# A two-layer decoder trunk on one core: one tiny quarter-array product behind the products that spread a norm's factor

## The chip, the cores and the metric

The kernel runs on one core of one Trainium2 chip. The metric is the device time of one execution in microseconds (us): the median of three runs before the change is 1049.05 us, the runs lie between 1049.01 and 1049.5 us. A profile is one execution, recorded instruction by instruction.

## What is computed

A trunk of two layers works on 256 tokens of width 1024. Each layer normalises the activations `h` by their root mean square, sends them through four token mixers, merges these by sigmoid gates, adds the result to `h`, normalises again for a feed-forward block with gate, and normalises a third time for a small gated block that is fed from a second input `p`.

```
def _rmsnorm(x, g):
    xf = x.astype(jnp.float32)
    y = xf * lax.rsqrt(jnp.mean(xf * xf, axis=-1, keepdims=True) + NORM_EPS)
    return (y * g.astype(jnp.float32)).astype(x.dtype)
...
for i in range(DEPTH):
    xn = _rmsnorm(h, norm_mix[i])
    u = xn @ w_in[i]
    ...
    h = h + (merged @ w_out[i]).astype(h.dtype)
    hn = _rmsnorm(h, norm_ffn[i])
    ff = (jax.nn.silu(hn @ w_ffn_gate[i]) * (hn @ w_ffn_up[i])) @ w_ffn_down[i]
    h = h + ff.astype(h.dtype)
    hp = _rmsnorm(h, norm_ple[i])
    ple = jax.nn.sigmoid(hp @ w_ple_gate[i]) * (p[i] @ w_ple_proj[i])
    h = h + ple.astype(h.dtype)
return _rmsnorm(h, norm_final)
```

## The kernel before

**Layout.** Features lie on the 128 partitions and the 256 tokens along the free axis. A weight tile of 128x1024 is loaded by one DMA of 512 KB from SyncE's queue (L210) and split in two parts: ScalarE writes the rounded part `wh` (L211), and VectorE, or for some tiles GpSimd, writes the rest `wl` (L212). There are four buffers for the raw tile and three for each part. The activations are split the same way into `xh` and `xl`.

**The big products.** One block of 128x128 weights times 128x256 activations takes three products that add up in PSUM: `wl` with `xh`, `wh` with `xl`, `wh` with `xh`. They are issued in `mm3` (L226, L227, L228), in `gemm_pair` where the last blocks of the input come late (L261, L262, L263), and in L430 to L432 for a token-major projection. All of them fill the whole array and stream 256 columns. In each layer the input projection (w_fm), the gates and branches (w_gate, w_branch), the output projection (w_out), the feed-forward (w_fg, w_fu, w_fd) and the last gate (w_pg) follow in this order on TensorE, each accumulation of 8, 16 or 22 blocks behind the other. TensorE executes in the order of its list.

**The small products.** The mixers work on chunks and heads with products on parts of the array (64x64, 128x64, 32x32 and others). They go through a helper `Front`, whose line L141 issues them ahead of the big ones as soon as they can be done, so that the big products fill the gaps.

**A norm.** The gain is multiplied into `xh` and `xl`, the factor `rsqrt(mean)` only after the products. `h_stat` makes this factor while TensorE goes on with products that don't need it yet. The squares are summed over partitions by products with a column of 1/1024 (L354, one column out). VectorE makes the inverse root (L285 to L299). Two products (L359) with the identity matrix spread the 2 x 128 factors over all partitions into 256 columns of a PSUM tile `pB` of 512 columns, and ScalarE copies them out (L365 of the old numbering, tile `rstd`). VectorE multiplies `rstd` into what leaves the projections. `h_stat` runs seven times: once for x, and in each layer behind the mixers (it makes the feed-forward's factor), behind the feed-forward (the last block's factor) and behind the last block (the next layer's mixers' factor, in the second layer that of the output).

**The order** of each engine's list is made by the framework when the kernel is built: it simulates the program and takes, among the instructions that are ready, the one with the lowest priority number. A change in one place can therefore move instructions elsewhere.

Of the kernel before, what the change touches and what calls it, by code (L numbers as in the profile page):

```python
# [32 lines left out]
P = 128  # L33
L = 2
T = 256
# [115 lines left out]
class Trunk:  # L151
# [193 lines left out]
                add(sq[:, 0], sq[:, 0], sq[:, 1])  # L345
                self.accs.pop()

    def h_stat(self, last=False):
        nc = self.nc
        ps = self.ps([P, 512], "pB")  # L350
        n = len(self.accs)
        for i, a in enumerate(self.accs):
            for tc_ in range(2):
                nc.tensor.matmul(ps[:, tc_:tc_ + 1], a[:, tc_ * P:(tc_ + 1) * P], self.inv_dm,  # L354
                                 start=i == 0 and tc_ == 0, stop=i == n - 1, skip_group_check=True)
        self.rt = self.rsqrt(ps[:, 0:2], 2, 1.0, EPS)
        bc = self.ps([P, 512], "pB")
        for tc_ in range(2):
            nc.tensor.matmul(bc[:, tc_ * P:(tc_ + 1) * P], self.rt[:, tc_:tc_ + 1].to_broadcast([P, P]), self.ident,  # L359
                             start=True, stop=True)  # L360
        self.rstd_ps = bc[:, None, :T].to_broadcast([P, 2, T])
        if last:
            return
        self.rstd = self.t([P, T], "rstd")
        nc.scalar.activation(self.rstd, bc[:, :T], AF.Copy)  # L365
        self.rstd_b = self.rstd[:, None, :].to_broadcast([P, 2, T])
# [820 lines left out]
    def body(self):  # L1187
        self.wcount = 0

        self.shared = False  # L1190
        self.tc.cur_priority += Front.AHEAD
        self.xp = [None] * 4
        self.stream = "B"

        self.lo_plan = list("VVVVV")
        self.setup()
        for p in range(4):
            for c in range(2):
                self.h_done(2 * p + c, lambda c: self.vec[0][:, V_MIX + c:V_MIX + c + 1], first=True)
            if p == 2:  # L1200
                self.ahead.append(self.w_tiles([self.ins["w_fm"][0, 7]], 2))
                self.nc.sync.dma_start(self.h[:, 6:8], self.ins["x"][:, 6:8])
        self.h_stat()
        for l in range(L):
            self.layer(l)

        hn = [self.g([P, 2, T], "A") for _ in range(4)]
        with self.tc.issue_after(self.last_sq.ins):
            for ch in range(8):
                self.nc.scalar.activation(hn[ch // 2][:, ch % 2], self.h[:, ch], AF.Copy,  # L1210
                                          scale=self.vec[0][:, V_NF + ch:V_NF + ch + 1])
        for p in range(4):
            o = self.g([P, 2, T], "B")
            for cs in (slice(0, 1), slice(1, 2)) if p == 0 else (slice(0, 2),):
                self.nc.vector.tensor_mul(o[:, cs], hn[p][:, cs], self.rstd_ps[:, cs])
                self.nc.sync.dma_start(self.out[:, 2 * p + cs.start:2 * p + cs.stop], o[:, cs])
# [34 lines left out]
    def layer(self, l):  # L1251
        nc = self.nc
# [28 lines left out]
        with lane("G"):  # L1281
            kv, ksw, q = self.nsa_in(l)
# [63 lines left out]
        for p in range(4):  # L1346
# [3 lines left out]
            for c, ps in parts:  # L1350
# [3 lines left out]
                for ts in halves:  # L1354
# [4 lines left out]
                    (G if adders[p] == "P" else V).tensor_add(hc, dc, hc)  # L1359
                    for i in range(n):  # L1360
                        self.h_done(2 * p + c + i, gcol, part=ts if len(halves) > 1 else None)
        self.h_stat(l + 1 == L)

    def residual(self, src, xs, gcol, tag=None):

        V = self.nc.vector
        for p in range(4):
            for c, ps in self.pair([src(2 * p + c) for c in range(2)], xs, 2 if p == 0 and len(xs) == 8 else 0, split=p == 3):
                n = ps.shape[1]
                hc = self.h[:, 2 * p + c:2 * p + c + n]  # L1370
                V.scalar_tensor_tensor(hc, ps, 0.5, hc, op0=OP.mult, op1=OP.add)
                for i in range(n):
                    self.h_done(2 * p + c + i, gcol, tag)
        self.h_stat()

# [89 lines left out]
```

## Time and profile before

| | |
|---|---|
| median of three runs | 1049.05 us |
| the profiled execution | 1048.63 us |
| its span, first to last instruction | 1046.9 us |
| TensorE products recorded | 9520 |
| VectorE busy | 738.5 us (71%) |
| ScalarE busy | 542.9 us (52%) |
| GpSimd busy | 240.2 us (23%) |
| DMA moved | 171.32 MB, mean 164 GB/s |

Busy time of an engine is the union of its instructions' records. A product's end is modelled by the profiler, and in a stream the records overlap (records of 0.28 us start 0.11 to 0.12 us apart); so what a product costs there is the distance between the starts of neighbours, not the length of its record. A product of two plain 32-bit operands appears as two records: L359 stands twice in each of the seven norms and shows 28 records. A row that names a helper's line (L141, L211, L226) collects all calls of the helper.

### The profile page before, as it was taken

The numbers are of one execution on the slowest core, as the hardware profiler recorded it, in microseconds if no ns is written. First come the engines' busy times: TensorE is split into PE (matmuls) and PEld (weight loads), VectorE is DVE, ScalarE is ACT, GpSimd is POOL, SyncE is SP. The second block draws the span as 40 slices with busy tenths as digits, with TensorE's granted clock in tenths as the row PEclk, the third lists the DMA queues.
The fourth block names the chain that finished last, engine by engine and source line by source line (L and its number), as shares of the span: only waits on it lengthen the run. The fifth ranks groups of instructions, "written<-read, shape, count | busy, mean of one in ns | idle before, by whom it ended". The sixth has DMA issues, their size and how long they took to land.

```text
span 1046.9 us, 22801 instructions
## 1 busy us (share of the span) xinstructions
PE 1026.3 (98%) x9520; PEld 986.2 (94%) x9520; DVE 738.5 (71%) x1216; ACT 542.9 (52%) x863; POOL 240.2 (23%) x154
## 2 busy tenths in 40 slices
PE   9999999999999999999899999999999999999996
PEld 9988988899999999999898999988999999999996
DVE  6888968766677667554878999576567676665456
ACT  6644555555654444444555545556556555444444
POOL 0000000044442242232510000000544432332322
PEclk9999999999999999999999999999999999999998
DMA  8654334256665656666544553333565656656551
GB/s 293 193 182 159 90 98 121 68 172 186 190 202 171 198 177 188 186 183 192 168 158 135 179 166 100 110 93 101 182 197 179 198 166 195 191 175 198 171 179 56
DMA packets 50502, 171.32 MB, mean 164 GB/s; under 512 B 5856, under 2 KB 6624, under 8 KB 50272
## 3 DMA queue, kind: packets, MB, share of 16 engines
q1 hardware_dynamic: 50112, 169.76, 52.2%
q8 instruction: 74, 1.21, 0.5%
q14 instruction: 28, 0.23, 0.1%
q10 hardware_dynamic: 288, 0.11, 0.0%
HBM read 168.80 MB, written 1.05 MB: 162 GB/s over the span
## 4 chain that ended last, share of the span: by engine, by line
PE 85%; DVE 9%; ACT 2%; issue 2%; DMA 1%; POOL 1%; DVEq 0%; ACTq 0%; POOLq 0%
PE mm L226 21%; PE mm L227 21%; PE mm L228 21%; PE pB L141 6%; PE pA L141 5%; DVE wl L212 3%; PE pA L226 2%; PE pA L227 2%; PE pA L228 2%; PE pA L262 1%; PE pA L261 1%; PE pA L263 1%; DMA T<-in_w_cmp_dram 1%; ACT wh L211 1%; DVE T L1358 1%
## 5 line engine op out<-in xcount | busy, mean ns | idle before, releaser
L211 ACT ACTIVATE wh<-wr 128x1024 fp32r<-128x1024 f32 (+3 forms) x314 | 325.6, 1040 | 347.0 <-PE mm L228 240.4
L212 DVE TENSOR_TENSOR wl<-wr,wh 128x1024 fp32r<-128x1024 f32 (+3 forms) x259 | 326.7, 1263 | 139.3 <-ACT wh L211 137.2
L226 PE MATMUL mm<-xh,wl 128*128 128x256 f32 x1472 | 415.4, 282 | 1.4 <-POOL wl L212 1.4
L227 PE MATMUL mm<-xl,wh 128*128 128x256 f32 x1472 | 413.6, 281 | 0.0
L228 PE MATMUL mm<-xh,wh 128*128 128x256 f32 x1472 | 413.5, 281 | 0.0
L228 PEld LDWEIGHTS mm<-xh,wh 128*128 128x128 f32 x1472 | 279.6, 190 | 2.4 <-issue 1.2
L226 PEld LDWEIGHTS mm<-xh,wl 128*128 128x128 f32 x1472 | 276.6, 188 | 5.0 <-POOL wl L212 1.8
L227 PEld LDWEIGHTS mm<-xl,wh 128*128 128x128 f32 x1472 | 276.6, 188 | 3.3 <-issue 2.1
L212 POOL TENSOR_TENSOR wl<-wr,wh 128x1024 fp32r<-128x1024 f32 (+1 forms) x55 | 130.5, 2375 | 265.5 <-ACT wh L211 265.5
L226 PE MATMUL mm<-A,wl 128*128 128x256 f32 x332 | 92.9, 280 | 0.0
L227 PE MATMUL mm<-A,wh 128*128 128x256 f32 x332 | 92.9, 280 | 0.0
L228 PE MATMUL mm<-A,wh 128*128 128x256 f32 x332 | 92.9, 280 | 0.0
L1337 POOL TENSOR_TENSOR B<-B,B 128x512 f32<-128x512 f32 x22 | 28.5, 1298 | 152.9 <-DVE B L1335 147.1
L228 PEld LDWEIGHTS mm<-A,wh 128*128 128x128 f32 x332 | 63.4, 191 | 0.0
L226 PEld LDWEIGHTS mm<-A,wl 128*128 128x128 f32 x332 | 62.3, 188 | 0.0
L227 PEld LDWEIGHTS mm<-A,wh 128*128 128x128 f32 x332 | 62.3, 188 | 0.0
L376 DVE TENSOR_TENSOR A<-B,A 128x512 fp32r<-128x512 f32 x18 | 36.8, 2045 | 33.3 <-ACT A L375 33.3
L141 PE MATMUL pA<-A,A 64*64 64x64 f32 (+3 forms) x1008 | 49.7, 223 | 1.2 <-DVE A L638 1.2
L141 PEld LDWEIGHTS pA<-A,A 64*64 64x64 f32 (+3 forms) x1008 | 41.6, 135 | 8.9 <-DVE A L638 1.6
L1249 POOL TENSOR_TENSOR M<-M,T 128x512 f32<-128x512 f32 x24 | 43.4, 1839 | 9.9 <-DVE T L1248 9.9
L226 PE MATMUL mm<-Y,wl 128*128 128x256 f32 x160 | 44.8, 280 | 0.0
L227 PE MATMUL mm<-Y,wh 128*128 128x256 f32 x160 | 44.4, 278 | 0.0
(391 smaller groups left out, 1742.1 us busy)
## 6 DMA issues: line engine op xcount, KB each, us to landing
wr<-in_w_gate_dram SPq DMA_DIRECT2D x64, 512.0 KB, 3.7
wr<-in_w_fm_dram SPq DMA_DIRECT2D x46, 512.0 KB, 3.7
wr<-in_w_fg_dram SPq DMA_DIRECT2D x44, 512.0 KB, 4.4
wr<-in_w_fu_dram SPq DMA_DIRECT2D x44, 512.0 KB, 3.7
wr<-in_w_fd_dram SPq DMA_DIRECT2D x32, 512.0 KB, 4.4
wr<-in_w_branch_dram SPq DMA_DIRECT2D x16, 512.0 KB, 4.1
wr<-in_w_out_dram SPq DMA_DIRECT2D x16, 512.0 KB, 3.7
wr<-in_w_pg_dram SPq DMA_DIRECT2D x16, 512.0 KB, 4.3
```

Source lines behind the costliest of these rows:

```text
L141: f(*args, **kw)
L211: nc.scalar.activation(hi[:, s], raw[:, s], AF.Copy)
L212: e.tensor_sub(lo[:, s], raw[:, s], hi[:, s])
L226: mm(out, wlo, xhi, start=start, stop=False)
L227: mm(out, whi, xlo, start=False, stop=False)
L228: mm(out, whi, xhi, start=False, stop=stop)
L261: mm(ps[:, c], lo, xs[k][0], start=c == 0 and k == 0, stop=False, skip_group_check=True)
L262: mm(ps[:, c], hi, xs[k][1], start=False, stop=False, skip_group_check=True)
L263: mm(ps[:, c], hi, xs[k][0], start=False, stop=k == n - 1, skip_group_check=True)
L376: self.nc.vector.tensor_sub(lo, src, hi)
L1249: self.nc.gpsimd.tensor_add(merged[p], merged[p], ths[p])
L1337: G.tensor_mul(up, th, up)
```

## The change

`h_stat` gets a parameter `steady`. Where it is set, one more product is issued behind the two products that spread the factor: 64 rows, 64 columns of weights (a quarter of the array at position 0, 0), both operands from the identity matrix, two columns out, written to columns 256 and 257 of the same PSUM tile `pB`, partitions 0 to 63. The copy to `rstd` reads columns 0 to 255, so nothing reads these two. `issue_after` places it behind the second of the two products. The parameter is set for x, behind the mixers of both layers, and behind the last block of the first layer: four times in all.

```
-    def h_stat(self, last=False):
+    def h_stat(self, last=False, steady=False):
...
         for tc_ in range(2):
-            nc.tensor.matmul(bc[:, tc_ * P:(tc_ + 1) * P], self.rt[:, tc_:tc_ + 1].to_broadcast([P, P]), self.ident,
+            bcast = nc.tensor.matmul(bc[:, tc_ * P:(tc_ + 1) * P], self.rt[:, tc_:tc_ + 1].to_broadcast([P, P]), self.ident,
                              start=True, stop=True)
+        if steady:
+
+            with self.tc.issue_after(bcast.ins):
+                q = slice(0, 64)
+                self.nc.tensor.matmul(bc[q, T:T + 2], self.ident[q, q], self.ident[q, :2], start=True, stop=True,
+                                      tile_position=(0, 0), skip_group_check=True)
...
-        self.h_stat()
+        self.h_stat(steady=True)
...
-        self.h_stat(l + 1 == L)
+        self.h_stat(l + 1 == L, l + 1 < L)
...
-        self.h_stat()
+        self.h_stat(steady=tag is None)
```

TensorE's list at the feed-forward's norm of the first layer, before (`pB_490` is the tile of the spread factor, `mm_503` the second pair of the gate's sums; the numbers at the end of names count tiles of the whole program):

```order
L227 MATMUL mm_503_4291<-xl_174,wh504_4293 128x256
L228 MATMUL mm_503_4291<-xh_173,wh504_4293 128x256
L359 MATMUL pB_490_4152<-cst_155,rs_y2B_489_4141 128x128 x2
L226 MATMUL mm_503_4291<-xh_173,wl504_4294 128x256
L227 MATMUL mm_503_4291<-xl_174,wh504_4293 128x256
```

And with the change, at the same place:

```order
L227 MATMUL mm_503_4293<-xl_174,wh504_4295 128x256
L228 MATMUL mm_503_4293<-xh_173,wh504_4295 128x256
L359 MATMUL pB_490_4153<-cst_155,rs_y2B_489_4142 128x128 x2
L365 MATMUL pB_490_4153<-cst_155 64x2
L226 MATMUL mm_503_4293<-xh_173,wl504_4296 128x256
L227 MATMUL mm_503_4293<-xl_174,wh504_4295 128x256
```

The tiny product (L365 of the new numbering) stands alone between the spreading products and the big products, which keep their order; the three other places look alike.

Elsewhere TensorE's list keeps its order but for some 40 of its rows in the two layers' mixers, most of them in the first. The largest move is in RWKV's part of the first layer (`pA_77`, `pA_78` are sums of its small products, `mm_209` a big one). Before:

```order
L141 MATMUL pA_77_664<-A_65_620,A_67_622 128x128
L141 MATMUL pA_77_664<-A_66_621,A_68_623 128x128
L226 MATMUL mm_209_1558<-xh_173,wl210_1561 128x256
L227 MATMUL mm_209_1558<-xl_174,wh210_1560 128x256
L228 MATMUL mm_209_1558<-xh_173,wh210_1560 128x256
L226 MATMUL mm_209_1558<-xh_173,wl210_1561 128x256
L227 MATMUL mm_209_1558<-xl_174,wh210_1560 128x256
L228 MATMUL mm_209_1558<-xh_173,wh210_1560 128x256
L141 MATMUL pA_78_677<-A_65_620,A_67_622 128x128
L141 MATMUL pA_78_677<-A_66_621,A_68_623 128x128
```

With the change, the rows around `pA_78`:

```order
L228 MATMUL mm_209_1559<-xh_173,wh210_1561 128x256
L226 MATMUL mm_209_1559<-xh_173,wl211_1592 128x256
L227 MATMUL mm_209_1559<-xl_174,wh211_1591 128x256
L141 MATMUL pA_78_678<-A_65_621,A_67_623 128x128
L141 MATMUL pA_78_678<-A_66_622,A_68_624 128x128
```

Between the two groups there now stand 21 big products instead of 6, so that the next weight tile (`wl211`) is begun ahead of `pA_78`. `pA_78` comes 21 products later in TensorE's list than before. VectorE and ScalarE change places of some instructions in the same stretch; GpSimd's and SyncE's lists stay as they were.

## The prediction

> **What bounds the kernel.** I read the page first, then the windows of the feed-forward, then the starts of single products. The page gives the span, the busy time and the chain that ended last:
>
> ```profile
> span 1046.9 us, 22801 instructions
> PE 1026.3 (98%) x9520; PEld 986.2 (94%) x9520; DVE 738.5 (71%) x1216; ACT 542.9 (52%) x863; POOL 240.2 (23%) x154
> PE 85%; DVE 9%; ACT 2%; issue 2%; DMA 1%; POOL 1%; DVEq 0%; ACTq 0%; POOLq 0%
> ```
>
> TensorE is the bound. A busy TensorE is not yet one at its best pace, so I look at a stage where it never waits: the two feed-forwards, between the spread of the norm's factor and the first sum of squares of the next norm. The windows' columns are stretch, its length, busy time with records, granted clock, DMA share and GB/s:
>
> ```profile
> 321.90:489.90 168.00, 168.00 (x1429) 1.00 0.61 183
> 837.00:1005.00 168.00, 168.00 (x1429) 1.00 0.60 183
> ```
>
> Both layers take the same time for the same products, at clock 1.00. Now the timeline of TensorE, start and length of each record. First a stretch of the gates (188 rows from first to last), then one of the feed-forward (181 rows):
>
> ```profile
> 231.77 0.28 PE L226 MATMUL mm<-xh,wl 128*128 128x256 f32 x1
> ...
> 252.96 0.28 PE L227 MATMUL mm<-xl,wh 128*128 128x256 f32 x1
> ```
> ```profile
> 341.73 0.28 PE L227 MATMUL mm<-xl,wh 128*128 128x256 f32 x1
> ...
> 362.93 0.28 PE L227 MATMUL mm<-xl,wh 128*128 128x256 f32 x1
> ```
>
> The same form of product starts every (252.96 - 231.77) / 187 = 113.3 ns in the gates and every (362.93 - 341.73) / 180 = 117.8 ns in the feed-forward. So there are **two paces**, 4.5 ns or 3.8% apart, at one and the same clock. The groups by line show them too, as mean record of 276 or 281 ns, and they show that the slow stretch is slow throughout (313 products of one kind, shortest, median and longest alike, with first and last start):
>
> ```profile
> L227 PE MATMUL mm<-xl,wh x313: 281/281/281, 322.3 to 432.5; 128*128 128x256 f32 x157
> L227 PE MATMUL mm<-xl,wh x74: 276/281/386, 23.9 to 55.8; 128*128 128x256 f32 x74
> L227 PE MATMUL mm<-xl,wh x73: 276/281/386, 541.3 to 584.9; 128*128 128x256 f32 x73
> ```
>
> The second and third row are the beginnings of the two layers' mixers: over half slow. **What sets the pace** shows at its changes. At the first norm the stream is fast until the spread of the factor (L359) and slow behind it:
>
> ```profile
> 23.35 0.28 PE L228 MATMUL mm<-xh,wh 128*128 128x256 f32 x1
> 23.47 0.28 PE L226 MATMUL mm<-xh,wl 128*128 128x256 f32 x1
> 23.58 0.60 PE L359 MATMUL pB<-cst,rs_y2B 128*128 128x128 f32 x4
> 23.94 0.36 PE L227 MATMUL mm<-xl,wh 128*128 128x256 f32 x1
> 24.14 0.28 PE L228 MATMUL mm<-xh,wh 128*128 128x256 f32 x1
> ...
> 24.97 0.28 PE L226 MATMUL mm<-xh,wl 128*128 128x256 f32 x1
> ```
>
> The starts ahead of it are 0.12 and 0.11 apart, those behind it (24.97 - 24.14) / 7 = 118.6 ns. I looked up all norms: behind the four spreads that the change touches the stream is slow each time, whatever it was before, and nothing in the feed-forward disturbs it again. A group of small products on quarters of the array does the opposite:
>
> ```profile
> 110.10 0.28 PE L227 MATMUL mm<-xl,wh 128*128 128x256 f32 x1
> ...
> 110.80 0.28 PE L227 MATMUL mm<-xl,wh 128*128 128x256 f32 x1
> 111.01 1.15 PE L141 MATMUL pA<-A,A 64*64 64x64 f32 x32
> ...
> 113.01 0.28 PE L430 MATMUL mm<-wl,xh 128*128 128x256 f32 x1
> ...
> 114.37 0.28 PE L430 MATMUL mm<-wl,xh 128*128 128x256 f32 x1
> ```
>
> Slow before (110.10 to 110.80, six starts, 117 ns), then (114.37 - 113.01) / 12 = 113.3 ns. Of the 16 places where a group that ends with 64*64 products of 64 columns is followed by enough big ones to tell, the stream is fast behind 14 and slow behind 2, a group at 142.6 us in the first layer and its twin in the second. Big products behind the former, five of one kind, in the groups by line:
>
> ```profile
> L227 PE MATMUL mm<-xl,wh x5: 281/281/388, 143.2 to 144.8; 128*128 128x256 f32 x5
> ```
>
> The change puts such a quarter-array product behind the spread.
>
> **The sum, against the profiled execution of 1048.63 us** (span 1046.9, 1.7 around it; the median of the runs is 0.4 higher).
>
> *Feed-forwards.* 168.00 us at 117.8 ns are 1426 products. At 113.3 ns they take 161.6 us: **-6.4 us in each layer, -12.8 in both**. I count on the fast pace to last, as it does in the gates where nothing comes between. Behind 489.9 us the sums of squares (L354) come, and their stretch to 500.4 stays as it was; were it fast as well, 10.4 us x 3.8% = 0.4 more in each layer.
>
> *Mixers' beginnings.* 31.9 and 43.6 us between first and last start, over half of it slow; all of it fast would be 1.2 and 1.7 us less, half 1.4 together. Part can return as longer waits, since TensorE waits for VectorE in the mixers (below). I take **-1.0**, with ends 0 and -2.9.
>
> *The tiny product.* No such product with two columns is in the trace. One spread is two products and four records, so this one is two records. From below: two more of L359's records, 0.11 us each, 0.22. From above: the short group of eight 64*64 records.
>
> ```profile
> 162.39 0.28 PE L228 MATMUL mm<-xh,wh 128*128 128x256 f32 x1
> 162.59 0.67 PE L141 MATMUL pA<-A,A 64*64 64x64 f32 x8
> 163.20 0.38 PE L226 MATMUL mm<-xh,wl 128*128 128x256 f32 x1
> 163.42 0.29 PE L227 MATMUL mm<-xl,wh 128*128 128x256 f32 x1
> ```
>
> From 162.39 to 163.42 are 1.03 us; without two ordinary starts of 0.113, 0.80 for eight records with the way in and out: the upper end. Eight records lie in 0.67, 0.084 each; without six of them 0.30 are left. I take 0.35, near that: **+1.4 for four places**, ends 0.9 and 3.2. The copy to `rstd` does not read the two columns, and on TensorE only big products stand behind. The Trainium skill, page TensorEngine Tiling (Array Packing), section Tiling Modes, says that changing the tiling mode drains the engine, which speaks against the change; the trace agrees in that the product behind the group has a long record (0.38 against 0.28), and that price is in the 0.30.
>
> *The moved rows.* `pA_78` comes 21 products later, 21 x 0.118 = 2.5 us. Its old records end at 79.85 + 1.16 = 81.0, VectorE takes them up for the last time here:
>
> ```profile
> 79.85 1.16 PE L141 MATMUL pA<-A,A 64*128 64x128 f32 x8
> 85.88 0.47 DVE L612 TENSOR_TENSOR A<-pA,cst 64x128 f32<-64x128 f32 x2
> ```
>
> That leaves 4.9 us, so the move costs nothing; without this cover it would be 2.5 us.
>
> Sum: -12.8 - 1.0 + 1.4 = -12.4, so 1036.2 us for the profiled execution and **1036.6 us** for the median. Ends: -12.8 - 0.8 - 2.9 + 0.9 = -15.6 or 1033.4 us, and -12.8 + 0 + 3.2 = -9.6 or 1039.4 us.
>
> **Does the rest keep up?** In the feed-forward's window (322 to 490 us), busy, mean and idle time with what ended it, and in the waits of TensorE:
>
> ```profile
> L211 ACT ACTIVATE wh<-wr 128x1024 fp32r<-128x1024 f32 (+1 forms) x61 | 63.1, 1034 | 73.8 <-PE mm L228 69.9 <-issue 2.5 <-ACT B L331 0.6
> L212 POOL TENSOR_TENSOR wl<-wr,wh 128x1024 fp32r<-128x1024 f32 (+1 forms) x16 | 37.4, 2339 | 42.0 <-ACT wh L211 42.0
> PE mm L226 <- POOL wl L212: 1.4, 2, 0.7
> PE pA L141 <- DVE A L638: 1.2, 2, 0.6
> ```
>
> ScalarE's splits wait for TensorE to free their buffers, 69.9 us, GpSimd waits for ScalarE: supply runs ahead and has to gain only 6.4 us. What could come of it is a wait like the two of 0.7 us on GpSimd's part in the gates, so 1 to 3 us in all, inside the ends above.
>
> **Rivals.**
> 1. *The tiny product does not set the pace.* The two exceptions behind 64*64 groups show that it hangs on more than the last form, and with two columns instead of 64 the way out may differ. Then only +1.4 and the moves remain: 1050.5 us, within 0.2% (about what a measurement of this kernel can tell from no change). For it: 2 of 16, and no product with two columns in the trace; against it: 14 of 16. The Trainium skill, TensorE: Matmul & The Clock Gate, section Back-to-back issue gap, gives one gap for 256 columns at full clock, 262 cycles of 2.4 GHz, by estimate 109 ns; by that rule nothing that went before would matter and this rival would hold. The trace shows 113.3 and 117.8 instead.
> 2. *One feed-forward only.* The surroundings are alike in both layers, but one could fall to the slow pace at a wait. Half of it: -6.4 + 1.4 - 0.5 = 1043.5 us.
> 3. *Slower: the moved chain has no cover.* RWKV's chain in the first layer ends at L638, for which TensorE already waits twice (1.2 us), so delay that reaches it is paid in full. If the pace stays slow and the 2.5 us of `pA_78` come through whole: 1049.05 + 1.4 + 2.5 = 1053 us. It decides once the cover of 4.9 us has shrunk below the 2.5, and makes the kernel slower only together with rival 1.
>
> **How the numbers follow.** Forecast, both feed-forwards fast: 0.70, own range 1033.4 to 1039.4. Rival 2: 0.10. Rival 1: 0.14. Rival 3: 0.06. The range from 1033 to 1044 holds the first two, 0.80. Faster is 0.70 + 0.10 = 0.80, same 0.14, slower 0.06.
>
> **What would show it.** Right: both windows of 168 us become some 161.6 us with mean records of 276 ns, the product behind the tiny one starts some 0.35 us later than now, TensorE's idle time in the feed-forward stays at 0. Wrong: records of 281 ns behind the tiny product (rival 1, in one layer rival 2), new waits of TensorE on `wl` in the feed-forward (supply), or a longer wait for L638 at about 133 us (rival 3).

## The result and the profile after

The changed kernel takes **1038.16 us** in the median of four runs (1037.06 to 1039.2); the kernel before took 1049.28 us beside it (1049.01 to 1049.69). The ratio is 0.9894, with a 95% interval of 0.9876 to 0.9911. The profiled execution took 1037.06 us, 11.57 us less than that of before. Line numbers above 359 are 6 larger than before; the tiny product is L365.

The page of the changed kernel, with span, busy time and the chain that ended last:

```profile
span 1035.3 us, 22817 instructions
PE 1016.1 (98%) x9528; PEld 975.6 (94%) x9528; DVE 735.6 (71%) x1216; ACT 542.1 (52%) x863; POOL 241.9 (23%) x154
PE 86%; DVE 9%; ACT 2%; issue 1%; DMA 1%; POOL 1%; DVEq 0%; ACTq 0%; POOLq 0%
```

Only the span tells of the gain: TensorE is busy 98% as before, with eight records more (four tiny products of two records each), and is 86% of the chain. So the same work went through at a better pace; the one wait that shrank is worth 0.9 us (below the table). The windows of the two feed-forwards say it outright, busy from end to end as before:

```profile
320.70:483.00 162.30, 162.30 (x1433) 1.00 0.64 190
831.00:993.20 162.20, 162.20 (x1432) 1.00 0.63 190
```

The timeline of TensorE at the norm of the first feed-forward, and the next norm's first sums (start, length, line):

```profile
320.73 0.28 PE L228 MATMUL mm<-xh,wh 128*128 128x256 f32 x1
320.84 0.60 PE L359 MATMUL pB<-cst,rs_y2B 128*128 128x128 f32 x4
321.38 0.27 PE L365 MATMUL pB<-cst 64*64 64x2 f32 x2
321.58 0.39 PE L226 MATMUL mm<-xh,wl 128*128 128x256 f32 x1
321.80 0.28 PE L227 MATMUL mm<-xl,wh 128*128 128x256 f32 x1
...
483.21 0.50 PE L354 MATMUL pB<-inv_dm,B 128*128 128x1 f32 x4
```

The same two marks in the profile of before:

```profile
321.74 0.60 PE L359 MATMUL pB<-cst,rs_y2B 128*128 128x128 f32 x4
...
490.01 0.50 PE L354 MATMUL pB<-inv_dm,B 128*128 128x1 f32 x4
```

From the spread to the sums it took 490.01 - 321.74 = 168.27 us and now takes 483.21 - 320.84 = 162.37. The groups by line give the reason, median records of 276 ns where 281 stood, in both layers; but the third and fourth row, the stretches behind the tiny products of the two mixers, are slow still:

```profile
L227 PE MATMUL mm<-xl,wh x313: 276/276/281, 321.8 to 427.9; 128*128 128x256 f32 x157
L227 PE MATMUL mm<-xl,wh x313: 276/276/281, 832.0 to 938.1; 128*128 128x256 f32 x157
L227 PE MATMUL mm<-xl,wh x43: 281/281/384, 24.2 to 39.2; 128*128 128x256 f32 x43
L227 PE MATMUL mm<-xl,wh x39: 281/281/384, 534.9 to 548.5; 128*128 128x256 f32 x39
```

Measured in the same way (first spread record to first record of the next sums), the stages of the two profiled executions are these (marks at 23.58, 308.72, 321.74, 490.01, 540.93, 823.81, 836.83 and 1005.11 us before, at 23.49, 307.82, 320.84, 483.21, 534.21, 818.00, 831.02 and 993.39 after; the rest takes in the time outside the span):

| stretch | before | after | difference |
|---|---|---|---|
| first layer's mixers and gates | 285.14 | 284.33 | -0.81 |
| first layer's feed-forward | 168.27 | 162.37 | -5.90 |
| second layer's mixers and gates | 282.88 | 283.79 | +0.91 |
| second layer's feed-forward | 168.28 | 162.37 | -5.91 |
| the rest | 144.06 | 144.20 | +0.14 |
| together | 1048.63 | 1037.06 | -11.57 |

The gain is that of the feed-forwards. The mixers gave nothing: less in one layer, more in the other. The first layer's -0.81 isn't pace either. TensorE waited 0.98 us there for the DMA of a mixer's weights (`w_cmp`, read into `T`); with the change this wait is 0.08 us, too short to be marked. Before, then after:

```profile
91.98 0.43 PE L141 MATMUL mm<-T,U 128*32 128x128 f32 x8 [0.98 <-DMA T<-in_w_cmp_dram]
```
```profile
90.78 0.43 PE L141 MATMUL mm<-T,U 128*32 128x128 f32 x8
```

Without these 0.90 us the mixers would have lost some 0.1 and 0.9 us.

### The profile page after: what moved, and what is told of

Same layout as the page of the kernel before. It is cut to its first block, busy times and chain, and to the rows that moved or that the text cites. A ratio compares the mean times of both kernels' runs of the same rounds, so it can differ in the third digit from the quotient of the medians.

```text
span 1035.3 us, 22817 instructions
## 1 busy us (share of the span) xinstructions
PE 1016.1 (98%) x9528; PEld 975.6 (94%) x9528; DVE 735.6 (71%) x1216; ACT 542.1 (52%) x863; POOL 241.9 (23%) x154
## 4 chain that ended last, share of the span: by engine, by line
PE 86%; DVE 9%; ACT 2%; issue 1%; DMA 1%; POOL 1%; DVEq 0%; ACTq 0%; POOLq 0%
PE mm L226 21%; PE mm L227 21%; PE mm L228 21%; PE pB L141 6%; PE pA L141 5%; DVE wl L212 2%; PE pA L226 2%; PE pA L227 2%; PE pA L228 2%; PE pA L261 1%; PE pA L262 1%; PE pA L263 1%; ACT wh L211 1%; DVE T L1364 1%; PE mm L438 1%
## 5 line engine op out<-in xcount | busy, mean ns | idle before, releaser
L211 ACT ACTIVATE wh<-wr 128x1024 fp32r<-128x1024 f32 (+3 forms) x314 | 325.4, 1040 | 333.8 <-PE mm L228 221.2
L226 PE MATMUL mm<-xh,wl 128*128 128x256 f32 x1472 | 412.6, 280 | 1.4 <-POOL wl L212 1.4
L228 PE MATMUL mm<-xh,wh 128*128 128x256 f32 x1472 | 411.1, 279 | 0.0
L227 PE MATMUL mm<-xl,wh 128*128 128x256 f32 x1472 | 411.0, 279 | 0.0
L226 PEld LDWEIGHTS mm<-xh,wl 128*128 128x128 f32 x1472 | 276.7, 188 | 5.3 <-POOL wl L212 1.8
L227 PEld LDWEIGHTS mm<-xl,wh 128*128 128x128 f32 x1472 | 277.1, 188 | 3.0 <-issue 1.4
L228 PEld LDWEIGHTS mm<-xh,wh 128*128 128x128 f32 x1472 | 276.7, 188 | 2.5 <-issue 1.1
L226 PE MATMUL mm<-A,wl 128*128 128x256 f32 x332 | 91.6, 276 | 0.0
L227 PE MATMUL mm<-A,wh 128*128 128x256 f32 x332 | 91.6, 276 | 0.0
L228 PE MATMUL mm<-A,wh 128*128 128x256 f32 x332 | 91.6, 276 | 0.0
L226 PEld LDWEIGHTS mm<-A,wl 128*128 128x128 f32 x332 | 62.3, 188 | 0.0
L227 PEld LDWEIGHTS mm<-A,wh 128*128 128x128 f32 x332 | 62.3, 188 | 0.0
L228 PEld LDWEIGHTS mm<-A,wh 128*128 128x128 f32 x332 | 62.3, 188 | 0.0
L226 PE MATMUL mm<-Y,wl 128*128 128x256 f32 x160 | 44.8, 280 | 0.0
L227 PE MATMUL mm<-Y,wh 128*128 128x256 f32 x160 | 44.5, 278 | 0.0
```

The lines of the kernel that those rows point to most:

```text
L211: nc.scalar.activation(hi[:, s], raw[:, s], AF.Copy)
L226: mm(out, wlo, xhi, start=start, stop=False)
L227: mm(out, whi, xlo, start=False, stop=False)
L228: mm(out, whi, xhi, start=False, stop=stop)
```

## The experiments

The questions: does the tiny product make the gain, and in which places; must it be a quarter of the array; and does such a product *set* the fast pace whatever runs ahead, or does it *turn* one pace into the other? The theory that the runs left standing was formed after the first four (E, where an expectation names it by a letter): **a quarter alone in the stream sets the fast pace, a whole-array product of two records turns the pace over**. Fast means 113.3 ns from start to start (records of 276 ns), slow 117.8 (281 ns). Medians come with range and number of runs; ratios are to the kernel before on the same chip. None of the added products is read. Rows of an experiment name `mm3`'s middle product L227 or L231, as the edit moved it.

### Only the feed-forwards

```
-        self.h_stat(steady=True)
+        self.h_stat()
...
-        self.h_stat(l + 1 == L, l + 1 < L)
+        self.h_stat(l + 1 == L)
```

> The tiny product stands behind the feed-forward's spread in both layers alone, not at the mixers' beginnings. If all of the gain is the feed-forward's pace (theory A), each feed-forward from the spread to the first sum of squares takes 162.4 us as with the change (168.3 before) and the whole time is 1037 to 1038.5 us, as with all four products. If the two products at the mixers' beginnings bring something that the profile of the change hides (rival), it is slower than the change by their share, 1 us or more.

Measured: 1036.87 us (1036.17 to 1038.7, six), ratio 0.9906 (0.9876 to 0.9937). Its groups by line, in a stretch of the first mixers and of each feed-forward:

```profile
L227 PE MATMUL mm<-xl,wh x40: 276/281/282, 24.9 to 38.7; 128*128 128x256 f32 x40
...
L227 PE MATMUL mm<-xl,wh x280: 276/276/276, 329.8 to 424.7; 128*128 128x256 f32 x140
...
L227 PE MATMUL mm<-xl,wh x281: 276/276/276, 839.7 to 934.9; 128*128 128x256 f32 x141
```

Two of the four tiny products carry the whole gain; those of the mixers bring nothing that can be measured. They cost some 0.8 us, and without them the wait for `w_cmp` is back at 0.74 us, so the two nearly cancel.

### The whole array, more columns, two of them

Three versions of the tiny product, in the same four places. Whole array:

```
-                q = slice(0, 64)
-                self.nc.tensor.matmul(bc[q, T:T + 2], self.ident[q, q], self.ident[q, :2], start=True, stop=True,
-                                      tile_position=(0, 0), skip_group_check=True)
+                self.nc.tensor.matmul(bc[:, T:T + 2], self.ident, self.ident[:, :2], start=True, stop=True,
+                                      skip_group_check=True)
```

> The tiny product keeps its four places and its two columns but fills the whole array (128 rows, 128 columns of weights). If a quarter of the array is what changes the pace (theory A, change of the array's shape), the feed-forwards stay at records of 281 ns and the time is about 1049.5 to 1050.5 us. If any further break of the stream does it (rival B, timing alone), they go to 276 ns and the time is about 1038 us.

A quarter with 64 columns:

```
-                self.nc.tensor.matmul(bc[q, T:T + 2], self.ident[q, q], self.ident[q, :2], start=True, stop=True,
+                self.nc.tensor.matmul(bc[q, T:T + 64], self.ident[q, q], self.ident[q, :64], start=True, stop=True,
```

> The quarter-array product has 64 columns instead of 2, as the mixers' small products have. If the number of columns decides why the mixers' beginnings stayed slow (rival C), they become fast: records of 276 ns at 24 to 57 us and behind 535 us, and up to 1.5 us less than the change. If the state ahead of it decides (theory D: slow ahead, fast behind; fast ahead, slow behind), mixers' beginnings stay at 281 ns, the feed-forwards at 276, and the time equals the change's within 1 us.

Two quarters, one behind the other:

```
-                self.nc.tensor.matmul(bc[q, T:T + 2], self.ident[q, q], self.ident[q, :2], start=True, stop=True,
-                                      tile_position=(0, 0), skip_group_check=True)
+                for i in range(2):
+                    self.nc.tensor.matmul(bc[q, T + 2 * i:T + 2 * i + 2], self.ident[q, q], self.ident[q, :2], start=True, stop=True,
+                                          tile_position=(0, 0), skip_group_check=True)
```

> Two tiny quarter products behind each other at each of the four places. If the state ahead is turned over by each of them (theory D, taken literally), feed-forwards return to 281 ns and the time to about 1050 us. If the first one's change of shape is what counts (theory A), feed-forwards stay at 276 ns and the time is the change's plus 4 times 0.06 to 0.11 us, 1038.4 to 1038.7. If the exact moment of re-entry decides (rival B), either can come, and mixers' beginnings may differ from feed-forwards.

Measured: 1036.6 us with the whole array (1036.28 to 1038.78, six; a seventh took 3501.51, see the last section), ratio 0.9913 (0.988 to 0.9945); 1037.08 with 64 columns (1035.35 to 1041.38, six), 0.9911 (0.9878 to 0.9944); 1037.96 with two (1036.94 to 1038.81, eight), 0.991 (0.9885 to 0.9934). Both feed-forwards are fast in all three. So **a quarter of the array isn't needed**, which already speaks against the reason that the prediction gave. The whole array does one thing that the quarter of two columns doesn't: the mixers' beginnings are fast, in both layers. The group of the second layer's stretch shows it for whole array (first) and two quarters (second):

```profile
L227 PE MATMUL mm<-xl,wh x26: 276/276/281, 540.8 to 550.7; 128*128 128x256 f32 x26
```
```profile
L227 PE MATMUL mm<-xl,wh x26: 276/281/383, 540.9 to 550.9; 128*128 128x256 f32 x26
```

That fits turning: at these norms the spread alone leaves the stream slow, and the whole-array product makes it fast. It doesn't show in the median: the beginnings are short.

The 64 columns gave what neither reading of their expectation has. The first layer's beginning is fast, the second's slow:

```profile
L227 PE MATMUL mm<-xl,wh x41: 276/276/387, 25.0 to 38.8; 128*128 128x256 f32 x41
...
L227 PE MATMUL mm<-xl,wh x25: 278/281/281, 540.9 to 550.7; 128*128 128x256 f32 x25
```

By the starts, the first stream came in fast and the second slow, so spread and quarter kept the pace in these two places and turned it in the feed-forwards.

### Twenty tiny products in each feed-forward

The kernel before, with one tiny product behind each accumulation of 48 big products, 20 in a feed-forward: quarters in the first layer, whole-array ones in the second.

```
+    def tiny(self, full):
+        bc = self.ps([P, 512], "pB")
+        with self.tc.issue_after(self.last_mm.ins):
+            if full:
+                self.nc.tensor.matmul(bc[:, :2], self.ident, self.ident[:, :2], start=True, stop=True)
+            else:
+                q = slice(0, 64)
+                self.nc.tensor.matmul(bc[q, :2], self.ident[q, q], self.ident[q, :2], start=True, stop=True,
+                                      tile_position=(0, 0), skip_group_check=True)
...
             self.gemm_pair(pg, [[ins["w_fg"][l, 2 * p + c]] for c in range(2)], self.xs(), 0 if p else 2)
+            if p:
+                self.tiny(l == 1)
```

> The kernel before, without a tiny product behind the spread, but with one behind each of 20 accumulations of 48 products in the feed-forward's gate and up projections, a quarter of the array in the first layer, the whole array in the second. Theory A (the change of shape restores the pace): the first layer is fast from the first one on and stays so, the second stays slow. Theory B (any break of the stream, the moment of re-entry decides): both layers change to the fast pace at some of the 20, and may fall back at others. Theory D (each turns the pace over): the pace alternates from one accumulation to the next in both. Price: 20 x 0.40 us = 8 us in the first layer and 20 x 0.22 = 4.4 us in the second; a fast stretch gains 48 x 4.5 ns = 0.22 us for each.

One execution, 1054.19 us. Two stretches between quarters in the first layer, then three successive ones between whole-array products in the second:

```profile
L227 PE MATMUL mm<-xl,wh x13: 276/276/276, 327.5 to 331.5; 128*128 128x256 f32 x13
L227 PE MATMUL mm<-xl,wh x13: 276/276/276, 333.3 to 337.4; 128*128 128x256 f32 x13
...
L227 PE MATMUL mm<-xl,wh x13: 276/276/276, 844.5 to 848.6; 128*128 128x256 f32 x13
L227 PE MATMUL mm<-xl,wh x13: 281/281/281, 850.2 to 854.5; 128*128 128x256 f32 x13
L227 PE MATMUL mm<-xl,wh x13: 276/276/276, 856.1 to 860.2; 128*128 128x256 f32 x13
```

The quarter found the stream slow once and fast 19 times and left it fast 20 times. The whole-array product turned it over 20 times out of 20. One and the same form of product at granted clock 1.00 thus holds either pace for as long as nothing else comes between. The Trainium skill, TensorE: Matmul & The Clock Gate, section Back-to-back issue gap, gives one gap per column count and calls it that of an isolated product; for streams in which each product has its own weight load it has figures for 128 and 512 columns alone. No single gap describes this stream.

The run also gives both prices in a plain stream. Timeline around a quarter, then around a whole-array product:

```profile
337.86 0.28 PE L228 MATMUL mm<-xh,wh 128*128 128x256 f32 x1
338.06 0.27 PE L238 MATMUL pB<-cst 64*64 64x2 f32 x2
338.27 0.39 PE L226 MATMUL mm<-xh,wl 128*128 128x256 f32 x1
338.49 0.28 PE L227 MATMUL mm<-xl,wh 128*128 128x256 f32 x1
...
849.06 0.28 PE L228 MATMUL mm<-xh,wh 128*128 128x256 f32 x1
849.18 0.28 PE L235 MATMUL pB<-cst 128*128 128x2 f32 x2
849.32 0.36 PE L226 MATMUL mm<-xh,wl 128*128 128x256 f32 x1
849.52 0.28 PE L227 MATMUL mm<-xl,wh 128*128 128x256 f32 x1
```

From L228 to the second product behind it are 338.49 - 337.86 = 0.63 us and 849.52 - 849.06 = 0.46; two ordinary fast starts are 0.23, so a quarter costs some 0.40 and a whole-array product 0.23 (0.43 and 0.25 with the few longer starts that follow). The quarter starts 0.20 behind its neighbour, the other 0.12. The Trainium skill, TensorEngine Tiling (Array Packing), section Tiling Modes, says that changing the tiling mode drains the engine; the trace agrees in that the quarter starts later, and it costs some 0.17 us more than the whole-array product.

### Two whole-array products, one of a single record, and one at every norm

If a whole-array product turns the pace over, two of them must bring the slow pace back. Two:

```
+                for i in range(2):
+                    self.nc.tensor.matmul(bc[:, T + 2 * i:T + 2 * i + 2], self.ident, self.ident[:, :2], start=True, stop=True,
+                                          skip_group_check=True)
```

> Two whole-array products with two columns behind each of the four spreads, where one made the stream fast at all four. Theory B with a count (each record of a break shifts the moment of re-entry by a fixed amount): some of the four places go back to 281 ns; if it is the feed-forwards, the time returns to 1049 us, if the mixers' beginnings, 1 us more than with one. If any extra product suffices: all four stay fast, and the time is that of one plus 4 x 0.22 us, about 1037.5 us.

One in bfloat16, behind the feed-forwards' spread alone:

```
+                self.nc.tensor.matmul(bc[:, T:T + 2], self.identb, self.identb[:, :2], start=True, stop=True,
+                                      skip_group_check=True)
```

> Behind the feed-forward's spread in both layers one whole-array product of bfloat16 operands, which is one record instead of two; nothing at the mixers' beginnings. If any extra product suffices, the feed-forwards are fast (about 1037 us). If what counts is where the break ends (theory B), one record less can leave them at 281 ns (about 1049.5 us).

The whole-array product of above behind every spread but the output's, so also behind the third norm of each layer:

```
-        self.h_stat(steady=tag is None)
+        self.h_stat(steady=True)
```

> One whole-array product with two columns behind every spread but the output's, also the one behind the feed-forward. Against one at four places: the stretch of the last block of each layer (w_pg, some 300 products) is fast where it happened to be slow, up to 0.9 us in the first layer and 0.4 in the second, for 2 x 0.22 us: 1036 to 1037 us, by theory B not better than 0.5 us than the four places.

Measured: two, 1049.11 us (1042.89 to 1050.81, ten), ratio 1.0004 (0.9979 to 1.003). The bfloat16 one, 1049.0 (1044.42 to 1050.02, ten), 1.0006 (0.9983 to 1.0028). Every norm, 1037.97 (1035.3 to 1044.99, twelve), 0.9925 (0.9901 to 0.9948). The feed-forwards by group, with the two products and then with the bfloat16 one:

```profile
L227 PE MATMUL mm<-xl,wh x270: 281/281/281, 329.8 to 424.9; 128*128 128x256 f32 x135
...
L227 PE MATMUL mm<-xl,wh x280: 276/276/276, 839.8 to 934.7; 128*128 128x256 f32 x140
```
```profile
L227 PE MATMUL mm<-xl,wh x270: 281/281/281, 329.8 to 424.9; 128*128 128x256 f32 x135
...
L227 PE MATMUL mm<-xl,wh x269: 281/281/281, 840.0 to 934.7; 128*128 128x256 f32 x135
```

So the gain isn't that of "a small product behind the spread": two undo it, and one of a single record brings nothing. But the second layer of the run with two is fast all the same, in an execution of 1042.89 us, one of three in ten at 1042 to 1045. Turning over is thus the rule for the whole array, perhaps not a law: the version at every norm had four of twelve runs at 1042 to 1045 as well, as if one feed-forward were slow; none of them was profiled. With quarters (the change, and the versions with feed-forwards only, 64 columns, two, and later) one run in 28 was above 1040 us.

### Quarters elsewhere

The same four products, not right behind the spread but alone in the stream, at the end of the next accumulation (written onto the kernel before):

```
             ps = self.in_pair(l, 2 * p, 2 if p == 3 else 0, "pA" if p in (3, 1) else "mm")
+            if p == 0:
+                self.tiny()
...
             self.gemm_pair(pg, [[ins["w_fg"][l, 2 * p + c]] for c in range(2)], self.xs(), 0 if p else 2)
+            if p == 1:
+                self.tiny()
```

> A quarter product at four places as in the change, but not right behind the spread: at the end of the next accumulation, between big products that run at the slow pace. Theory E, from the 40 products of the run before: alone in a running stream a quarter product always leaves the fast pace behind it, a whole-array one turns the pace over. Then all four places are fast, the mixers' beginnings too (281 ns up to the product, 276 behind it), and the feed-forwards take 0.1 to 0.3 us more than the change's 162.4; in all 0 to 1.5 us less than the change, 1036.5 to 1038. If the mixers' beginnings are slow for another reason than the place (rival F, what is different there), they stay at 281 ns.

Measured: 1036.98 us (1035.54 to 1037.55, four), ratio 0.9892 (0.9861 to 0.9923). In all four places the stream is slow ahead and fast behind, in the mixers too, where the change itself leaves it slow. The group ahead of the first product and the one behind it (which starts at 27.69):

```profile
L227 PE MATMUL mm<-xl,wh x7: 281/281/281, 24.5 to 26.7; 128*128 128x256 f32 x7
...
L227 PE MATMUL mm<-xl,wh x7: 276/276/286, 27.4 to 29.8; 128*128 128x256 f32 x7
```

So the neighbour counts: behind a spread the mixers' quarter left the stream slow, alone it leaves it fast. The next run put quarters alone into the middle of an accumulation's products (between L226 and L227) in the first layer, and a spread with a quarter into the second layer, in turn at an end and in a middle:

```
         first = mm(out, wlo, xhi, start=start, stop=False)
+        if self.probe and not start and not stop:
+            self.probe -= 1
+            if not self.probe:
+                self.tiny(first)
...
+        with self.tc.issue_after(behind.ins):
+            if self.spread:
+                for i in range(2):
+                    behind = mm(bc[:, i * P:(i + 1) * P], self.rt[:, i:i + 1].to_broadcast([P, P]), self.ident, start=True, stop=True)
+        with self.tc.issue_after(behind.ins):
+            q = slice(0, 64)
+            mm(bc[q, T:T + 2], self.ident[q, q], self.ident[q, :2], start=True, stop=True, tile_position=(0, 0),
+               skip_group_check=True)
```

> The kernel before with quarter products in the feed-forwards: in the first layer 20 alone, in the middle of an accumulation, between L226 and L227 of one block, where the mixers' spreads stand; in the second layer 20 behind a copy of the two spreading products, by turns at the end of an accumulation (as in the feed-forward) and in the middle of one (as at the mixers' beginnings). Theory E: the first layer is fast behind all 20. If the place within the accumulation decides: the first layer slow, in the second layer fast behind the ends and slow behind the middles. If the pace ahead decides behind a spread (theory D): the second layer alternates, fast behind slow and slow behind fast.

One execution, 1068.46 us. Alone in the middle of an accumulation, the quarter left the stream fast 19 times out of 19, but it also found it fast each time; the first of the 20 stands right behind the norm's own spread and went from slow to fast. With a spread ahead, it turned the pace each time: slow ahead and fast behind at the ends, fast ahead and slow behind in the middles. Place and pace ahead are thus mixed, and the next run takes them apart: spread and quarter 20 times at ends in the first layer, 20 times in middles in the second (same `tiny`, `self.spread` set in both, calls by layer).

> The kernel before with 20 copies of the two spreading products and a quarter product in each feed-forward: in the first layer all at ends of accumulations, in the second all in the middle of one. In the run before, place and pace ahead went together (ends entered slow, middles fast), so they could not be told apart. If the pace ahead decides (theory D, for the quarter product behind a spread): both layers alternate, fast behind slow and slow behind fast. If the place decides: the first layer fast behind all 20, the second slow behind all 20.

One execution, 1077.18 us. Three successive stretches at ends and two at middles, by group:

```profile
L231 PE MATMUL mm<-xl,wh x16: 276/276/283, 326.8 to 331.9; 128*128 128x256 f32 x16
L231 PE MATMUL mm<-xl,wh x16: 281/281/281, 333.1 to 338.4; 128*128 128x256 f32 x16
L231 PE MATMUL mm<-xl,wh x15: 276/276/281, 340.0 to 344.8; 128*128 128x256 f32 x15
...
L231 PE MATMUL mm<-xl,wh x13: 276/276/281, 852.0 to 856.1; 128*128 128x256 f32 x13
L231 PE MATMUL mm<-xl,wh x15: 281/281/281, 857.6 to 862.6; 128*128 128x256 f32 x15
```

The pace turned 40 times out of 40, in either kind of place (one of the 40 has the norm's own spread ahead of it as well). The place is out. The pace ahead alternates here along with the accumulation (gate, up, gate, up), so this run alone can't part those two; the change's own places do, since they fit the pace and don't alternate: fast to slow in both mixers, slow to fast in both feed-forwards, and just so in the version with two quarters.

### The spread alone

What the pair does without its quarter: 20 spreads at ends in the first layer, 20 spreads with one whole-array product in the second.

```
+        if self.full:
+            with self.tc.issue_after(behind.ins):
+                mm(bc[:, T:T + 2], self.ident, self.ident[:, :2], start=True, stop=True, skip_group_check=True)
```

> The kernel before with 20 copies of the two spreading products at ends of accumulations in each feed-forward: alone in the first layer, with a whole-array product of two columns behind them in the second. By the profiles so far a spread alone leaves the slow pace behind it: the first layer stays slow behind nearly all 20 (2 to 4 of them fast, as 3 of 10 executions of an even number of extra products gave one fast feed-forward). With one whole-array product behind it: fast behind most of them, whatever the pace ahead, as in 4 of 4 places of the profile with it; if the pace ahead decides, they alternate.

Inconclusive. The one execution took 2610.76 us, with every big product of the kernel slowed, also those far from the added ones (last section). Neither of the two paces occurs in it. What a spread alone does can be read from the other profiles, all but this one: 34 of their norms' spreads stand in a running stream, without a wait ahead and without an added product behind. At the mixers' beginnings 13 went from fast to slow and one from slow to fast. At the feed-forwards' norms all 8 went from slow to slow. At the third norm of the second layer 10 went from slow to fast and 2 from fast to slow. One of these ten, in the profile of after at 1011.13 us, by the groups ahead of it and behind it:

```profile
L227 PE MATMUL pA<-U,wh x7: 281/281/281, 1006.8 to 1009.6; 128*128 128x256 f32 x7
...
L227 PE MATMUL mm<-U,wh x8: 276/276/277, 1011.8 to 1014.9; 128*128 128x256 f32 x8
```

So a spread alone doesn't always leave the slow pace behind it, as the expectation took from fewer places: it turned the pace 26 times in 34, and the feed-forwards' norms are the exception.

That is also the comparison on which the change rests. At the feed-forwards' norms a spread alone left the stream slow 8 times out of 8; with one or two quarters right behind it, it left it fast 9 times out of 9. One whole-array product behind the spread gave the other pace than the spread alone does at the same norm, in all nine such places of the two versions that have it. One of these is the third norm of the second layer, which went from slow to slow with it.

## Why the prediction was right, point by point

- **What bounds the kernel, and the two paces.** Right. TensorE stays the bound at the same 98%, and the pace of its products is what changed.
- **Feed-forwards, -6.4 us each, with 0.35 back for the tiny product.** Right in place and nearly in size: -5.90 and -5.91 with the price included, where -6.05 was forecast. The fast pace lasts over the whole feed-forward, as counted on.
- **The tiny product, 0.35 us.** It is 0.40: from L228 at 320.73 to the second product behind are 1.07 us, where the prediction's rows of the first norm have 24.14 - 23.47 = 0.67. The two bounds, 0.22 and 0.80, held. All four cost 1.6, not 1.4.
- **Mixers' beginnings, -1.0 us.** This is the step that failed. They entered their norm fast and left it slow, with the tiny product as without it. The reading behind it, that a quarter-array product leaves the stream fast (14 of 16 places), holds where such a product stands alone (43 of 43 in three runs, though only 5 of them found the stream slow). Right behind a spread the pair of two columns turned the pace over instead (the change's four places, and 40 of 40), and with 64 columns it kept it in both mixers. In the mixers the change's pair did what the spread alone does there. The feed-forwards gained because the sums of squares ahead of their norm had left the stream slow; had they left it fast, the same product would have brought nothing, as in the mixers. That last step is argued from the turns in short stretches; no run made a whole feed-forward enter fast.
- **Where the rest went.** With -1.0 for the beginnings and +0.7 for their two products the mixers were to give -0.3; they gave -0.81 and +0.91, so +0.1, and that with the 0.90 us of the wait for `w_cmp`, which the sum didn't have. In the second layer's gates TensorE waits for GpSimd's `wl` at 764.8 as it did before, but behind this wait its products are slow until 797, where they were fast. And behind the first feed-forward the second group of squares, at 493.79, finds the stream slow and leaves it slow, where before, at 500.59, it found it slow and left it fast; so w_pg runs slow as well. Two rows each, after and then before:

```profile
L227 PE MATMUL mm<-Y,wh x32: 281/281/281, 783.0 to 793.9; 128*128 128x256 f32 x32
...
L227 PE MATMUL pA<-U,wh x5: 281/281/281, 495.2 to 496.6; 128*128 128x256 f32 x5
```
```profile
L227 PE MATMUL mm<-Y,wh x38: 276/276/281, 764.0 to 799.5; 128*128 128x256 f32 x38
...
L227 PE MATMUL pA<-U,wh x5: 276/276/276, 502.0 to 503.3; 128*128 128x256 f32 x5
```

  By the starts, 258 slow products from 740 us to the mark at 818.00 (5 in the same stretch before) and 190 from 493.79 to 534.21 (1 before), at 4.5 ns each 1.2 and 0.9 us; the second is made up by shorter waits. So breaks that the change didn't touch, entered at the same pace, left another pace behind them. The sum, made stage by stage, left that out, and why they did is open.
- **The moved rows and the supply.** Right in that they cost nothing that shows. The waits that the prediction named are those of before, two on GpSimd's `wl` and two for RWKV's L644 (L638 before), word for word the same sums:

```profile
PE mm L226 <- POOL wl L212: 1.4, 2, 0.7
...
PE pA L141 <- DVE A L644: 1.2, 2, 0.6
```

  What the prediction didn't see is that the wait for `w_cmp` nearly goes. Leaving the slowed execution of the last experiment aside, it is 0.6 to 1.0 us in the six profiles with nothing added at the first mixers' beginning and at most 0.14 us in the seven with a product there. Whether the moved rows or the delay itself do this is not shown.
- **Rivals.** That the tiny product doesn't set the pace fell for the feed-forwards but was half true in its reason: the outcome hangs on more than the last product's form. One feed-forward only did not happen here; the whole-array version at every norm has runs of the size that it would give. The slower case didn't come: `pA_78` had its cover.

No version beats the change beyond doubt. The medians of 1036.6 to 1037.0 of three versions were measured beside other runs of the kernel before (1048.37 and 1048.62 us in the median, against 1049.28 beside the 1038.16); their ratios (0.9892 to 0.9913) lie within each other's intervals, and the change's 0.9894 lies within all three. The quarter moved to the end of an accumulation has the one advantage that, in the places tried, its effect didn't depend on the pace ahead.

**What stays open:** what in TensorE holds the two paces; why a spread and a quarter together turn the pace, when the quarter alone sets it; why 64 columns kept it in the mixers; and why a spread alone turns the pace at most norms but leaves it slow at the feed-forwards'.

## What to carry to other kernels

Where an engine is busy without a gap, compare the distances between starts of one and the same instruction in different stages: a difference of 4% at one clock is time that no wait shows, and here it was decided by what stood at the stage's entry. A small product that nothing reads can be worth its 0.4 us at the entry of a long stretch of big ones; measure it in that place and more than once, since it can as well turn a fast stream slow. In a sum by stages, ask also in which state each stage hands the engine to the next.

## What the runs showed of the hardware

- **A product of two columns can turn the pace of the 48 big ones behind it, and the next turns it back**, 20 times in a row at one granted clock, so the stream carries something over that no record shows.
- **The kernel before has executions of two lengths.** On the chip of the runs with two, bfloat16 and every norm, 9 of its 29 were at 1042.8 to 1045.2 us and 20 at 1047.3 to 1052; on the chip of the first four experiments 4 of its 18 were at 1041.1 to 1045.7. The distance is that of one fast feed-forward (5.9 us), and the profiled execution of the same length with two products (1042.89) has just one. That those of the kernel before have one too is likely, but none was profiled.
- **Two executions were 2.5 and 3.4 times as long** (2610.76 and 3501.51 us), of kernels that differ little from others that ran as expected. In the profile of the first, between two of the added spreads, the window shows TensorE busy throughout at a recorded clock of 1.00, and the group's records of 537 ns stand where 276 or 281 are usual:

```profile
784.50:798.90 14.40, 14.40 (x50) 1.00 0.25 73
```
```profile
L231 PE MATMUL mm<-xl,wh x16: 531/537/540, 785.0 to 798.5; 128*128 128x256 f32 x16
```

  The 45 starts from the first to the last of these 16 (three products each) are (798.5 - 785.0) / 45 = 300 ns apart, 2.5 times the slow pace. Of the engines only TensorE is slower: VectorE is busy for 739.2 us and ScalarE for 541.9, as in the profile of before (738.5 and 542.9). The cause is open. The Trainium skill, TensorE: Matmul & The Clock Gate, section Seeing it yourself, warns that recorded clock events have been unreliable and that the gate has been seen stuck low; a recorded 1.00 beside such distances fits the first, and no run here shows the second.
